# Regrouping the last units of a mixture-of-experts layer: three experts in the sixth unit, two on column tiles in the last, and the overflow branch moved

## The chip, the cores and the metric

The kernel runs on one core of a Trainium2 chip. The metric is the device time of one execution in microseconds. Before the change the median of three runs is 446.82 us (442.83, 446.82 and 448.70).

## What is computed

One decoder layer on 256 tokens of width 1024. A token mixer (sparse attention beside an mLSTM) and a layer norm come first. The change lies in the second half, the hierarchical mixture of experts, and in the last layer norm:

```python
for e in range(N_EXPERTS):                    # 16 experts, 1024 -> 512 -> 1024, f32
    hdn = jax.nn.silu(t @ w_gate[e]) * (t @ w_up[e])
    out = out + combine[:, e:e + 1] * (hdn @ w_down[e])   # combine: 0 but for a token's two experts
x = layer_norm(ALPHA * x + out, ln2_g, ln2_b)
```

Only two experts of each token have a weight above 0, so an expert's product needs only its own tokens.

## The kernel before

**Units.** After routing, the experts are ranked by how many tokens they have. Each gets a fixed number of rows, and experts are packed into units of 128 rows, one matmul output tile each. Units 1 and 2 hold experts 0 to 3 with 64 rows each. The other twelve experts follow `PLAN` in the order of `ORDER`: unit 3 has two experts of 64 rows, unit 4 four of 32, unit 5 one of 128, unit 6 four of 32, unit 7 one of 32. The constant `ALONE` marks the last. Tokens that do not fit in any of these rows are counted in `nex`; a loop behind a branch, `beyond()` (L1314), would compute them. In the runs shown its body does not run.

**One unit.** `onehot` (L1093, VectorE) builds the selection matrix OH from the token positions, `back` (L1134) transposes it (tile `poht`) and takes the routing weights (`pcw`), `gather` (L1115) multiplies the token matrix (a high and a low part, `x1h` and `x1l`, in fp32r) with OH and so collects the unit's tokens in `xg` (tile `pxg`). OH and `xg` are made for two units at a time. `gate` (L1171) makes `psg` and ScalarE's silu of it, `up_h` (L1184) makes `psu` and VectorE's `h`. `hidden_T` (L1195) transposes `h` (`pht`, `hT`), `down` (L1236) multiplies it with the down weights (`psd`) and writes two parts of `y`, and `combine` (L1250) scatters `y` back onto the tokens (`pcomb`) and adds it to the accumulator `x`. Each of the products of gate, up and down reads 2 MB of weights for each expert. A unit of four experts of 32 rows places each on its own column tile of TensorE, at output rows 0, 32, 64 and 96.

**The unit that stands alone.** With a single expert of 32 rows, three of four column tiles would be empty. `product_alone` (L1151) therefore splits the contraction instead: four slices of 128 input channels lie on the four column tiles at once (tile `pp`), and a product with the matrix `fold` adds the four partial sums (directly for the gate, after ScalarE's copy `part`; within the transpose for the rest). `down_part` (L1207) does the same with the hidden channels, in three cuts of the columns (`CUTS`: 512, 320 and 192), so that the sums for the last layer norm (`bn_stats`, tile `bst`) can start on the first cut.

**What sets the order.** Weights go through a ring of 20 slots of 1 MB. SyncE issues every load in the order of `loads_in_order`: for odd positions the gate weights of a unit, the down weights of the unit before it, then its up weights; for even positions down first. A load waits until the load eight places before it has landed, and until its slot is free. The down weights of the last unit are loaded by column cuts, 512 columns first, then 320, then 192. On TensorE the instructions run in the order in which the scheduler lists them. In the loop of L1358 a unit's `down` is placed behind the next unit's gate or gather. For the last unit, the order is: `combine` of unit 5, the branch `beyond()`, `onehot`, `back`, `gather` of 32 columns, and only then `down` of unit 6, whose `combine` comes at the end of the loop body.

Of the kernel before, what the change touches and what calls it, by code (L numbers as in the profile page):

```python
# [17 lines left out]
P = 128  # L18
D = 1024
KC = D // P  # L20
S = 256
# [8 lines left out]
PLAN = ((128,), (64, 64), (32, 32, 32, 32), (32, 32, 32, 32), (32,))  # L30
ORDER = (1, 2, 0, 3, 4)
ALONE = (32,)
# [27 lines left out]
def tile_layer(ctx: ExitStack, tc: tile.TileContext, x, w_in, cst, rows, toep, w_uk, w_uv,  # L60
# [1032 lines left out]
    def onehot(us):  # L1093

        OH = wk.tile([P, NB, 2 * P], F32R, tag="oh", name="oh")
        for u, (key, es, ws, pm, cm) in enumerate(us):
            if ws == ALONE:

                for b in range(NB):
                    nc.vector.tensor_scalar(OH[:, b, :P].rearrange("p (e j) -> p e j", e=4), iota1[:, :32].unsqueeze(1).to_broadcast([P, 4, 32]),  # L1100
                                            pm[:, b, 0:1], None, op0=ALU.is_equal)
# [13 lines left out]
    def gather(OH, n, kcs=range(KC), xg=xg):  # L1115

        for k0 in kcs[::2]:
            ps = tp_tile("pxg").rearrange("p (k t) -> p k t", k=2)
            for k in range(2):
                for i, (b, part) in enumerate(((0, x1h), (0, x1l), (1, x1h), (1, x1l))):  # L1120
                    nc.tensor.matmul(ps[:, k, :n], part[:, b, (k0 + k) * P:(k0 + k + 1) * P], OH[:, b, :n],  # L1121
                                            start=i == 0, stop=i == 3)
# [10 lines left out]

    def back(OH, u, unit):  # L1134

        cm = unit[4]
        us = slice(u * P, (u + 1) * P)
        pt = tp_tile("poht")
        for b in range(NB):
            nc.tensor.transpose(pt[:, b * P:(b + 1) * P], OH[:, b, us].bitcast(F32), ident)  # L1140
        OHT = wk.tile([P, S], F32R, tag="sc", name="oht", bufs=2)
        nc.scalar.copy(OHT, pt[:, :S])  # L1142
        pc = sm_tile("pcw")
        for b in range(NB):
            nc.tensor.matmul(pc[:, 0:len(unit[1])], OH[:, b, us].bitcast(F32), cm[:, b, :], start=b == 0, stop=b == 1)
        cw = wk.tile([P, 1], F32, tag="cw", name="cw", bufs=2)
        for i, ss, _ in ((0, slice(0, P), {}),) if unit[2] == ALONE else slots(unit):
# [23 lines left out]
    def gate(unit, u, psg=None):  # L1171
        if unit[2] == ALONE:
            part = wk.tile([P, 512], F32, tag="w2", name="part", bufs=2)
            nc.scalar.copy(part, product_alone(unit, 0))
# [5 lines left out]
        sg = wk.tile([P, 512], F32, tag="w2", name="sg", bufs=2)  # L1180
        nc.scalar.activation(sg, psg, AF.Silu)  # L1181
        return sg

    def up_h(unit, u, sg, cw):  # L1184
        if unit[2] == ALONE:
            psu = product_alone(unit, 1)
# [3 lines left out]
        h = wk.tile([P, 4, P], F32, tag="w2b", name="h", bufs=2)  # L1190
        nc.vector.scalar_tensor_tensor(h.rearrange("p j q -> p q j"), psu.rearrange("p (q j) -> p q j", j=4), cw[:, 0:1],  # L1191
# [3 lines left out]
    def hidden_T(h, alone=False):  # L1195
        pt = tp_tile("pht").rearrange("p (j t) -> p j t", j=4)
        for j in range(4):
            if alone:

                nc.tensor.matmul(pt[:, j, :], h[:, j, :], fold, start=True, stop=True)  # L1200
            else:
                nc.tensor.transpose(pt[:, j, :], h[:, j, :], ident)  # L1202
        hT = wk.tile([P, 4, P], F32, tag="hT", name="hT")
# [3 lines left out]
    def down_part(unit, hT, y, c0, n):  # L1207
# [12 lines left out]
    def y_parts(y, psd, c0, n):  # L1220
        ys = slice(c0, c0 + n)
        nc.scalar.copy(y[:, 0, ys], psd)  # L1222
        nc.vector.tensor_tensor(y[:, 1, ys], psd, y[:, 0, ys].bitcast(F32), op=ALU.subtract)  # L1223
# [12 lines left out]
    def down(unit, h):  # L1236
        hT, y = hidden_T(h), y_tile()
# [120 lines left out]
    for n, unit in enumerate(units):  # L1358
        if waits:
            if unit[2] == ALONE:  # L1360
# [16 lines left out]
        if n == 0:  # L1377
# [42 lines left out]
            fold_xg = wk.tile([P, P + KC * 32], F32, tag="wrs", name="fold_xg")  # L1420
            fold = fold_xg[:, :P]
            xga = fold_xg[:, P:].rearrange("p (k t) -> p k t", k=KC)
            nc.vector.tensor_reduce(fold[:, 0:32], ident.rearrange("p (i s) -> p s i", i=4), AX.X, ALU.add)
            nc.vector.tensor_copy(fold[:, 32:].rearrange("p (i s) -> p i s", i=3), fold[:, 0:32].unsqueeze(1).to_broadcast([P, 3, 32]))
        waits = (y, prev[2]) if n % 2 and n + 1 < NUNITS else None
        if prev and not waits:
# [99 lines left out]
```

## Time and profile before

| | before |
|---|---|
| median of 3 runs | 446.82 us |
| the profiled execution, device time | 444.41 us |
| its span | 442.7 us |
| TensorE busy | 419.2 us (95%) |
| VectorE busy | 226.1 us (51%) |
| ScalarE busy | 163.1 us (37%) |
| bytes moved | 137.28 MB, mean 310 GB/s |
| granted TensorE clock, mean | 0.972 of 2.4 GHz |

The profiled execution's own time, 444.41 us, is its span of 442.7 us and 1.7 us around it. PE stands for TensorE's matmuls, PEld for its weight loads, DVE for VectorE, ACT for ScalarE, SP for SyncE, whose queue issues the loads. A plain f32 matmul leaves two records in the trace, one of fp32r a single one. Ends of matmuls are modelled, so the records of a stream overlap; where a product's length matters, it is read from start to start.

### The profile page before, as it was taken

To read this page: it belongs to the slowest core of one execution; us is meant where nothing else is said; L and a number is where in the kernel's file an instruction comes from. 1 tells how busy PE (TensorE), PEld (TensorE's weight loads), DVE (VectorE), ACT (ScalarE), POOL (GpSimd) and SP (SyncE) were. 2 spreads that over 40 slices of the span, in tenths; PEclk is the share of its full clock that TensorE was granted. 3 is DMA by queue.
4 is the path that set the end of the run, shared out by engine and by line. 5 is a ranking of instruction groups with operands and counts; after the bars stand their busy time and mean duration, and the time that the engine had idled before them with its cause. 6 is when DMAs were issued, how large, how long until landed. Compare 5 with 4: busy or idle time off the path is not lost. (4 is left out here: it accounts for less than half of the span.)

```text
span 442.7 us, 7254 instructions
## 1 busy us (share of the span) xinstructions
PE 419.2 (95%) x2832; PEld 300.5 (68%) x2832; DVE 226.1 (51%) x493; ACT 163.1 (37%) x294; POOL 45.4 (10%) x74
## 2 busy tenths in 40 slices
PE   6999999999999999999999999999998999979980
PEld 6999996999999999999964434433334443426230
DVE  3698996499647756677582614204032202311247
ACT  4558556765766434454554011210112100101210
POOL 6326205041010001110000000000000000000001
PEclk8999999999999999999999999999999999995996
DMA  8973770796296878669687999999999999999962
GB/s 254 340 254 97 291 236 10 238 377 231 99 376 205 283 273 289 190 209 382 229 321 286 375 386 390 423 419 423 420 423 421 419 423 417 423 418 419 414 224 95
DMA packets 48519, 137.28 MB, mean 310 GB/s; under 512 B 3539, under 2 KB 32355, under 8 KB 36451
## 3 DMA queue, kind: packets, MB, share of 16 engines
q1 hardware_dynamic: 47394, 135.75, 81.0%
q10 hardware_dynamic: 1088, 1.05, 0.8%
q8 instruction: 23, 0.38, 0.4%
q14 instruction: 14, 0.11, 0.1%
HBM read 135.74 MB, written 1.05 MB: 309 GB/s over the span
## 5 line engine op out<-in xcount | busy, mean ns | idle before, releaser
L249 PE MATMUL accT<-xh,split 128*128 128x256 f32 (+1 forms) x264 | 75.6, 286 | 0.0
L253 PE MATMUL accT<-xh,split 128*128 128x256 f32 (+1 forms) x264 | 75.1, 284 | 0.3 <-DVE split L240 0.3
L252 PE MATMUL accT<-xl,split 128*128 128x256 f32 (+1 forms) x264 | 75.1, 284 | 0.0
L240 DVE TENSOR_TENSOR split<-raw,split 128x1024 fp32r<-128x1024 f32 (+2 forms) x52 | 63.9, 1234 | 18.4 <-ACT split L239 18.3
L239 ACT CAST split<-raw 128x1024 fp32r<-128x1024 f32 (+2 forms) x59 | 59.2, 1012 | 32.3 <-PE accT L253 10.1
L253 PEld LDWEIGHTS accT<-xh,split 128*128 128x128 f32 (+1 forms) x264 | 50.2, 190 | 0.5 <-DVE split L240 0.5
L249 PEld LDWEIGHTS accT<-xh,split 128*128 128x128 f32 (+1 forms) x264 | 50.2, 190 | 0.4 <-PE pl L589 0.2
L1243 PE MATMUL psd<-we,hT 128*32 128x512 f32 (+2 forms) x240 | 48.6, 638 | 1.7 <-ACT hT L1204 1.7
L252 PEld LDWEIGHTS accT<-xl,split 128*128 128x128 f32 (+1 forms) x264 | 50.2, 190 | 0.0
L1166 PE MATMUL psu<-we,xg 128*32 128x512 f32 (+2 forms) x240 | 47.3, 594 | 0.4 <-DMA we<-in_w_up_dram 0.4
L1166 PE MATMUL psg<-we,xg 128*32 128x512 f32 (+2 forms) x232 | 47.1, 596 | 0.0
L1223 DVE TENSOR_TENSOR y<-psd,y 128x512 fp32r<-128x512 f32 x12 | 8.3, 692 | 61.9 <-ACT y L1222 61.9
L1243 PEld LDWEIGHTS psd<-we,hT 128*32 128x32 f32 (+2 forms) x240 | 14.8, 132 | 30.8 <-issue 27.6
L1166 PEld LDWEIGHTS psu<-we,xg 128*32 128x32 f32 (+2 forms) x240 | 14.5, 126 | 28.9 <-issue 27.6
L1191 DVE SCALAR_TENSOR_TENSOR h<-psu,cw,sg 128x512 f32<-128x512 f32 x6 | 6.7, 1120 | 51.7 <-PE psu L1166 39.1
L1166 PEld LDWEIGHTS psg<-we,xg 128*32 128x32 f32 (+2 forms) x232 | 14.0, 125 | 24.1 <-issue 21.8
L1465 POOL TENSOR_TENSOR nm<-nm,nhalf 128x2 f32<-128x2 f32 x1 | 1.8, 1772 | 211.0 <-DVE nm L1466 211.0
L1142 ACT CAST oht<-poht 128x256 fp32r<-128x256 f32 x7 | 2.6, 371 | 53.6 <-PE pcomb L1229 28.3
L1222 ACT CAST y<-psd 128x512 fp32r<-128x512 f32 x12 | 7.0, 585 | 41.0 <-PE psd L1243 41.0
L1230 DVE TENSOR_TENSOR x<-x,pcomb 128x512 f32<-128x512 f32 (+2 forms) x30 | 17.9, 644 | 6.6 <-PE pcomb L1229 6.6
L240 POOL TENSOR_TENSOR split<-raw,split 128x1024 fp32r<-128x1024 f32 x7 | 17.5, 2505 | 20.0 <-ACT split L239 19.9
L1229 PE MATMUL pcomb<-y,oht 128*128 128x512 f32 (+2 forms) x60 | 18.6, 436 | 0.2 <-ACT y L1217 0.2
(356 smaller groups left out, 814.0 us busy)
## 6 DMA issues: line engine op xcount, KB each, us to landing
we<-in_w_up_dram SPq DMA_DIRECT2D x32, 1024.0 KB, 11.5
we<-in_w_gate_dram SPq DMA_DIRECT2D x31, 1024.0 KB, 11.1
we<-in_w_down_dram SPq DMA_DIRECT2D x31, 1024.0 KB, 15.2
raw<-in_w_in_dram SPq DMA_DIRECT2D x18, 1024.0 KB, 7.0
raw<-in_w_out_dram SPq DMA_DIRECT2D x4, 1024.0 KB, 4.9
raw<-in_w_up_a_dram SPq DMA_DIRECT2D x2, 1024.0 KB
raw<-in_w_up_m_dram SPq DMA_DIRECT2D x2, 1024.0 KB, 6.0
raw<-in_w_in_dram SPq DMA_DIRECT2D x2, 528.0 KB
```

The costliest lines, as they stand in the source:

```text
L239: a = nc.scalar.copy(hi, raw)
L240: b = (nc.gpsimd if pool else nc.vector).tensor_tensor(lo, raw, hi.bitcast(F32), op=ALU.subtract)
L249: i = nc.tensor.matmul(o, ah, bh, start=start, stop=False)
L252: nc.tensor.matmul(o, ah, bl, start=False, stop=False)
L253: return nc.tensor.matmul(o, al, bh, start=False, stop=stop)
L1166: last = nc.tensor.matmul(ps[ss, :], xg[:, kc, u * P + ss.start:u * P + ss.stop], wtiles[unit[0], wi, i, hf][kc % 4], start=kc == 0, stop= ...
L1191: nc.vector.scalar_tensor_tensor(h.rearrange("p j q -> p q j"), psu.rearrange("p (q j) -> p q j", j=4), cw[:, 0:1], sg.rearrange("p (q j) ...
L1222: nc.scalar.copy(y[:, 0, ys], psd)
L1223: nc.vector.tensor_tensor(y[:, 1, ys], psd, y[:, 0, ys].bitcast(F32), op=ALU.subtract)
L1229: i = [nc.tensor.matmul(pc, o, v, start=i == 0, stop=i == len(parts) - 1) for i, (o, v) in enumerate(parts)]
L1230: nc.vector.tensor_tensor(acc[:, b, ys], acc[:, b, ys], pc, op=ALU.add)
L1243: nc.tensor.matmul(psd[nh][ss, :], hT[:, j, ss], wtiles[unit[0], 2, i, hf][j % 2][:, nh * 512:nh * 512 + 512], start=j == 0, stop=j == 3, ...
```

## The change

Unit 6 holds three experts of 32 rows (96 rows; the gather of the pair of units 5 and 6 has 224 columns), and unit 7, the last, two experts of 32 rows. For it, `product_pair` lays two slices of the contraction of each of the two experts on the four column tiles (tile rows 0 and 32 for the first expert, 64 and 96 for the second), and `fold` adds the two slices. The down weights of the last unit are now six column cuts, two experts by three. In the loop, `down` and `combine` of unit 6 now come ahead of the branch, and the gather, of 64 columns, behind it.

```diff
-PLAN = ((128,), (64, 64), (32, 32, 32, 32), (32, 32, 32, 32), (32,))
+PLAN = ((128,), (64, 64), (32, 32, 32, 32), (32, 32, 32), (32, 32))
...
-    def product_alone(unit, wi):
+    def product_pair(unit, wi):
         pp = acc_tile("pp")
         for hf in range(2):
-            for k in range(4):
-                t = slice(k * 32, k * 32 + 32)
-                nc.tensor.matmul(pp[t, :], xga[:, hf * 4 + k, :], wtiles[unit[0], wi, 0, hf][k], start=hf == 0, stop=hf == 1,
-                                 tile_position=(0, k * 32))
-            consumed(1)
+            for k in range(0, 4, 2):
+                for i in range(2):
+                    for r in range(2):
+                        t = i * 64 + r * 32
+                        nc.tensor.matmul(pp[t:t + 32, :], xg[:, hf * 4 + k + r, i * 32:i * 32 + 32], wtiles[unit[0], wi, i, hf][k + r],
+                                         start=hf * 4 + k == 0, stop=hf * 4 + k == 6, tile_position=(0, t))
+            consumed(2)
...
-        for j in range(4):
-
-            t = slice(j * 32, j * 32 + 32)
-            i = nc.tensor.matmul(psd[t, :], hT[:, j, t], wtiles[unit[0], 2, 0, nh][j][:, o:o + n], start=True, stop=True, tile_position=(0, j * 32))
-            first = first or i
+        for j in range(0, 4, 2):
+            for e in range(2):
+                for r in range(2):
+
+                    q = e * 64 + r * 32
+                    i = nc.tensor.matmul(psd[q:q + 32, :], hT[:, j + r, q:q + 32], wtiles[unit[0], 2, e, nh][j + r][:, o:o + n],
+                                         start=j == 0, stop=j == 2, tile_position=(0, q))
+                    first = first or i
...
-            if unit[2] == ALONE:
+            if unit[2] == PAIR:
                 combine(*waits)
+                combine(down(*prev[:2]), prev[2])
                 beyond()
             OH = onehot(units[n:n + 2])
-            if unit[2] != ALONE:
+            if unit[2] != PAIR:
                 combine(*waits)
         OHT, cw = back(OH, n % 2, unit)
-        if waits and unit[2] == ALONE:
-            gather(OH, 32, xg=xga)
-        if waits:
+        if waits and unit[2] == PAIR:
+            gather(OH, 64, twice=True)
+        elif waits:
             y = down(*prev[:2])
-            if unit[2] != ALONE:
-                gather(OH, 2 * P)
+            gather(OH, P + rows_of(units[n + 1]))
```

On TensorE, around the branch. These are the rows before the change, from the up product of unit 6 (`psu`, four column tiles) to the branch on `nex`:

```order
L1243 MATMUL psd<-we,hT 128x512 x8
L1166 MATMUL psu<-we,xg 32x512
L1229 MATMUL pcomb<-y,oht 128x512 x8
L1166 MATMUL psu<-we,xg 32x512 x31
L1317 TENSOR_LOAD nex
L1320 COMPARE_AND_BRANCH
```

and these the rows of the same place now:

```order
L1258 MATMUL psd<-we,hT 128x512 x8
L1175 MATMUL psu<-we,xg 32x512
L1244 MATMUL pcomb<-y,oht 128x512 x8
L1175 MATMUL psu<-we,xg 32x512 x23
L1213 MATMUL pht<-ident,h 128x96 x4
L1258 MATMUL psd<-we,hT 32x512 x24
L1244 MATMUL pcomb<-y,oht 128x512 x8
L1332 TENSOR_LOAD nex
L1335 COMPARE_AND_BRANCH
```

The up product has 24 matmuls in place of 32, and the transpose, the down product and the eight `pcomb` of unit 6 moved in front of the branch.

On TensorE, behind the last gather. Before, `down` of unit 6 comes first (`pht`, `psd` of 32 matmuls), then the last unit's products (`pp`, `psg` by `fold`, `pht`, `psd` in cuts) with the `pcomb` of unit 6 between them:

```order
L1202 MATMUL pht<-ident,h 128x128 x4
L1243 MATMUL psd<-we,hT 32x512 x32
L1157 MATMUL pp<-we,fold_xg 32x512 x8
L1229 MATMUL pcomb<-y,oht 128x512 x4
L1176 MATMUL psg<-part,fold_xg 128x512
L1157 MATMUL pp<-we,fold_xg 32x512 x8
L1229 MATMUL pcomb<-y,oht 128x512 x4
L1200 MATMUL pht<-fold_xg,h 128x128 x4
L1215 MATMUL psd<-we,hT 32x512 x4
L1215 MATMUL psd<-we,hT 32x320 x4
L1229 MATMUL pcomb<-y,oht 128x512 x2
L1215 MATMUL psd<-we,hT 32x192 x4
```

and now:

```order
L1166 MATMUL pp<-we,xg 32x512 x16
L1185 MATMUL psg<-part,fold 128x512
L1166 MATMUL pp<-we,xg 32x512 x16
L1211 MATMUL pht<-fold,h 128x128 x4
L1228 MATMUL psd<-we,hT 32x512 x8
L1228 MATMUL psd<-we,hT 32x320 x8
L1244 MATMUL pcomb<-y,oht 128x512 x2
L1228 MATMUL psd<-we,hT 32x192 x8
```

Nothing of unit 6 stands behind the gather any more, and each product of the last unit has twice the matmuls.

On SyncE, the last weight loads ahead of the branch, before (the gate's second half, the two of up, the cuts of down; `ISA` computes an address):

```order
L130 DMA we<-in_w_gate_dram 128x2048
L130 ISA
L130 DMA we<-in_w_up_dram 128x2048
L130 ISA
L130 DMA we<-in_w_up_dram 128x2048
L130 ISA
L130 DMA we<-in_w_down_dram 128x4x512
L130 ISA
L130 DMA we<-in_w_down_dram 128x4x320
L130 ISA
L130 DMA we<-in_w_down_dram 128x4x192
```

and now, from the last load of up (four of gate and three of up stand ahead of it):

```order
L130 DMA we<-in_w_up_dram 128x2048
L130 ISA
L130 DMA we<-in_w_down_dram 128x4x512
L130 ISA
L130 DMA we<-in_w_down_dram 128x4x512
L130 ISA
L130 DMA we<-in_w_down_dram 128x4x320
L130 ISA
L130 DMA we<-in_w_down_dram 128x4x320
L130 ISA
L130 DMA we<-in_w_down_dram 128x4x192
L130 ISA
L130 DMA we<-in_w_down_dram 128x4x192
```

The number of bytes is the same; 12 MB instead of 6 MB belong to the last unit, and 4 MB instead of 2 MB come in column cuts.

## Rows read from the trace of the kernel before

**Rows 1.** Page part 2, 40 equal slices: granted clock, DMA share, GB/s
```profile
PEclk8999999999999999999999999999999999995996
DMA  8973770796296878669687999999999999999962
GB/s 254 340 254 97 291 236 10 238 377 231 99 376 205 283 273 289 190 209 382 229 321 286 375 386 390 423 419 423 420 423 421 419 423 417 423 418 419 414 224 95
```

**Rows 2.** Timeline of TensorE: start us, us, what, count [idle before]
```profile
306.91 7.07 PE L1166 MATMUL psg<-we,xg 128*32 128x512 f32 x62
313.91 0.66 PE L1202 MATMUL pht<-ident,h 128*128 128x128 f32 x4
...
352.97 7.03 PE L1166 MATMUL psg<-we,xg 128*128 128x512 f32 x16
359.83 7.03 PE L1166 MATMUL psu<-we,xg 128*128 128x512 f32 x16
...
376.39 7.13 PE L1243 MATMUL psd<-we,hT 128*128 128x512 f32 x16
383.46 1.04 PE L1166 MATMUL psu<-we,xg 128*32 128x512 f32 x2
384.43 2.24 PE L1229 MATMUL pcomb<-y,oht 128*128 128x512 f32 x8
386.61 4.49 PE L1166 MATMUL psu<-we,xg 128*32 128x512 f32 x36
391.48 3.62 PE L1166 MATMUL psu<-we,xg 128*32 128x512 f32 x26 [0.39 <-DMA we<-in_w_up_dram]
```

**Rows 3.** SyncE's issues of weight loads, timeline from 390 us
```profile
394.05 2.81 SPq L130 DMA_DIRECT2D we<-in_w_gate_dram  x2
399.01 2.81 SPq L130 DMA_DIRECT2D we<-in_w_up_dram  x2
403.96 14.17 SPq L130 DMA_DIRECT2D we<-in_w_down_dram  x3
424.16 0.85 SPq L1460 DMA_DIRECT2D lnr<-in_rows_dram  x2
```

**Rows 4.** Line 130 from 380 us: down loads, ns each, first and last start
```profile
L130 SPq DMA_DIRECT2D we<-in_w_down_dram x8: 333/333/8788, 381.6 to 409.3; - x8
```

**Rows 5.** Page part 6: the loads of the two later cuts, KB, us to landing
```profile
we<-in_w_down_dram SPq DMA_DIRECT2D x1, 640.0 KB, 19.2
...
we<-in_w_down_dram SPq DMA_DIRECT2D x1, 384.0 KB, 17.3
```

**Rows 6.** Timeline of TensorE, last unit: waits for its gate and up weights
```profile
416.31 0.30 PEld L1157 LDWEIGHTS pp<-we,fold_xg 128*32 128x32 f32 x8 [0.56 <-DMA we<-in_w_gate_dram]
...
419.43 1.07 PE L1157 MATMUL pp<-we,fold_xg 128*32 128x512 f32 x8
421.30 1.07 PE L1157 MATMUL pp<-we,fold_xg 128*32 128x512 f32 x8 [0.80 <-SPq L1320]
```

**Rows 7.** The chain that ended last, by time (extract): start us, us, what
```profile
397.90 6.85 PE pxg L1121 x32
404.75 0.97 PE pht L1202 x4
...
406.43 9.37 PE psd L1243 x64
415.81 1.72 PE pp L1157 x16
...
422.49 1.15 DVE h L1191
423.68 1.17 PE pht L1200 x8
...
425.56 1.11 PE psd L1215 x8
```

**Rows 8.** Timeline of VectorE: adds, h, one-hot, and the first add of the end
```profile
385.20 2.48 DVE L1230 TENSOR_TENSOR x<-x,pcomb 128x512 f32<-128x512 f32 x4 [0.33 <-PE pcomb L1229]
395.14 1.10 DVE L1191 SCALAR_TENSOR_TENSOR h<-psu,cw,sg 128x512 f32<-128x512 f32 x1 [7.46 <-PE psu L1166]
396.55 0.48 DVE L1100 TENSOR_SCALAR oh<-iota,pmP 128x128 fp32r<-128x128 f32 x2 [0.31 <-DVEq L1320]
...
428.50 0.69 DVE L1230 TENSOR_TENSOR x<-x,pcomb 128x512 f32<-128x512 f32 x1 [3.77 <-PE pcomb L1229]
```

**Rows 9.** Windows: stretch, us, busy of PE, PEld, DVE, ACT, POOL, clock, DMA, GB/s
```profile
396.00:397.00 1.00, 0.02 (x1) 0.05 (x1) 0.69 (x3) 0.00 (x0) 0.00 (x0) 1.00 0.99 401
397.00:398.00 1.00, 1.00 (x8) 1.00 (x8) 0.09 (x2) 0.37 (x1) 0.00 (x0) 0.73 0.96 401
...
411.00:412.00 1.00, 1.00 (x12) 0.24 (x8) 0.00 (x0) 0.00 (x0) 0.00 (x0) 0.94 0.94 393
```

**Rows 10.** Timeline of TensorE: gather of 256 columns, first and last of seven matmuls
```profile
339.08 0.28 PE L1121 MATMUL pxg<-oh,x1l 128*128 128x256 f32 x1
...
339.79 0.28 PE L1121 MATMUL pxg<-oh,x1l 128*128 128x256 f32 x1
```

**Rows 11.** Groups by form from 240 us (busy us, mean ns): weight loads of column tiles
```profile
L1166 PEld LDWEIGHTS psu<-we,xg 128*32 128x32 f32 x128 | 4.4, 109 | 11.9 <-issue 10.6 <-DMA we<-in_w_up_dram 1.3
```

More of the change, by code (lines that the diff above doesn't have):

```diff
@@ L1113, in scaled, with gather, of @@
                 nc.vector.tensor_scalar(xg[:, k + 1, :n], odd, ln1gq[:, k + 1:k + 2], ln1bq[:, k + 1:k + 2], op0=ALU.mult, op1=ALU.add))
-    def gather(OH, n, kcs=range(KC), xg=xg):
+    def gather(OH, n, kcs=range(KC), twice=False):
+        def of(b):
+            return OH[:, b, :2 * n].rearrange("p (e i j) -> p e i j", e=2, i=2)[:, :, 0, :] if twice else OH[:, b, :n]
         for k0 in kcs[::2]:
@@ L1132, in slots, with rows_of @@
             q += w
+    def rows_of(unit):
+        return P if unit[2] == PAIR else sum(unit[2])
     def back(OH, u, unit):
-        cm = unit[4]
-        us = slice(u * P, (u + 1) * P)
+        cm, r = unit[4], rows_of(unit)
+        us = slice(u * P, u * P + r)
         pt = tp_tile("poht")
         for b in range(NB):
-            nc.tensor.transpose(pt[:, b * P:(b + 1) * P], OH[:, b, us].bitcast(F32), ident)
-        OHT = wk.tile([P, S], F32R, tag="sc", name="oht", bufs=2)
-        nc.scalar.copy(OHT, pt[:, :S])
+            nc.tensor.transpose(pt[:r, b * P:(b + 1) * P], OH[:, b, us].bitcast(F32), ident)
+        OHT = wk.tile([P, S], F32R, tag="sc", name="oht", bufs=2)[:r]
+        nc.scalar.copy(OHT, pt[:r, :S])
         pc = sm_tile("pcw")
         for b in range(NB):
-            nc.tensor.matmul(pc[:, 0:len(unit[1])], OH[:, b, us].bitcast(F32), cm[:, b, :], start=b == 0, stop=b == 1)
+            nc.tensor.matmul(pc[:r, 0:len(unit[1])], OH[:, b, us].bitcast(F32), cm[:, b, :], start=b == 0, stop=b == 1)
         cw = wk.tile([P, 1], F32, tag="cw", name="cw", bufs=2)
-        for i, ss, _ in ((0, slice(0, P), {}),) if unit[2] == ALONE else slots(unit):
+        for i, ss, _ in [(i, slice(i * 64, i * 64 + 64), {}) for i in range(2)] if unit[2] == PAIR else slots(unit):
             nc.vector.tensor_copy(cw[ss, :], pc[ss, i:i + 1])
         return OHT, cw
-    def product_alone(unit, wi):
+    def product_pair(unit, wi):
         pp = acc_tile("pp")
         for hf in range(2):
-            for k in range(4):
-                t = slice(k * 32, k * 32 + 32)
-                nc.tensor.matmul(pp[t, :], xga[:, hf * 4 + k, :], wtiles[unit[0], wi, 0, hf][k], start=hf == 0, stop=hf == 1,
-                                 tile_position=(0, k * 32))
-            consumed(1)
+            for k in range(0, 4, 2):
+                for i in range(2):
+                    for r in range(2):
[3 more added lines that the diff above has]
+            consumed(2)
         return pp
@@ L1171, in gate @@
     def gate(unit, u, psg=None):
-        if unit[2] == ALONE:
+        if unit[2] == PAIR:
             part = wk.tile([P, 512], F32, tag="w2", name="part", bufs=2)
-            nc.scalar.copy(part, product_alone(unit, 0))
+            nc.scalar.copy(part, product_pair(unit, 0))
             psg = acc_tile("psg")
@@ L1179, in gate @@
             product(psg, unit, 0, u)
-        sg = wk.tile([P, 512], F32, tag="w2", name="sg", bufs=2)
-        nc.scalar.activation(sg, psg, AF.Silu)
+        sg = wk.tile([P, 512], F32, tag="w2", name="sg", bufs=2)[:rows_of(unit)]
+        nc.scalar.activation(sg, psg[:rows_of(unit)], AF.Silu)
         return sg
     def up_h(unit, u, sg, cw):
-        if unit[2] == ALONE:
-            psu = product_alone(unit, 1)
+        if unit[2] == PAIR:
+            psu = product_pair(unit, 1)
         else:
@@ L1221, in y_parts @@
         ys = slice(c0, c0 + n)
-        nc.scalar.copy(y[:, 0, ys], psd)
-        nc.vector.tensor_tensor(y[:, 1, ys], psd, y[:, 0, ys].bitcast(F32), op=ALU.subtract)
+        r = y.shape[0]
+        nc.scalar.copy(y[:, 0, ys], psd[:r])
+        nc.vector.tensor_tensor(y[:, 1, ys], psd[:r], y[:, 0, ys].bitcast(F32), op=ALU.subtract)
     def combine_part(y, OHT, b, c0, n):
@@ L1236, in down @@
     def down(unit, h):
-        hT, y = hidden_T(h), y_tile()
+        hT, y = hidden_T(h), y_tile()[:rows_of(unit)]
         psd = [acc_tile("psd") for _ in range(2)]
@@ L1418, in tile_layer @@
                             nc.vector.scalar_tensor_tensor(acc[:, b, ns], pgb, ALPHA, acc[:, b, ns], op0=ALU.mult, op1=ALU.add)
[L1420 to L1424, printed above, removed]
+            fold = wk.tile([P, P], F32, tag="wrs", name="fold")
+            fv, iv = (t.rearrange("p (e r j) -> p e r j", e=2, r=2) for t in (fold, ident))
+            for r in range(2):
+                nc.vector.tensor_tensor(fv[:, :, r, :], iv[:, :, 0, :], iv[:, :, 1, :], op=ALU.add)
         waits = (y, prev[2]) if n % 2 and n + 1 < NUNITS else None
-        if prev and not waits:
+        if prev and not waits and unit[2] != PAIR:
             combine(y, prev[2])
```

28 lines of the change are left out of this document (15 added, 13 removed).

## The prediction

> **What bounds the kernel now.** I read the page's slices first. From the 26th slice to the 38th the DMA engines are full at about 420 GB/s [rows 1], so from some 277 us on (25 slices of 11.07 us) the weights arrive at a fixed pace, and only an idle stretch of the queue could move their end. Next I read who waits at the end. TensorE works without a gap up to 391 us, where unit 6's up product waits 0.39 us for its weights [rows 2]. The last unit's gate product then waits for a load that lands at 416.3, its up product for one that lands at 421.3 [rows 6]. Two loads of 1 MB between these give 2.5 us a load. SyncE is far ahead: it issues these loads between 394 and 410 [rows 3], the last cut at 409.3 [rows 4], and that lands 17.3 later [rows 5], at 426.6. Behind 421.3 comes a chain that waits for no load: the second half of up to 422.4, `h`, the transpose by `fold`, `psd` at 425.56 [rows 6, 7], the first add into the accumulator at 428.50 [rows 8]. From there to the end VectorE's adds and the layer norm take what they take, unchanged. So the change is worth what it does to that first add.
>
> One more thing is to be seen. The granted clock is 1.2 GHz from 397.7 to about 411.1 [rows 9]. Ahead of the fall TensorE stood idle from 395.1 to 397.0, and then came the gather, whose 32 matmuls of 32 columns took 6.85 us [rows 7]. Ahead of the rise it had run `psd` since 406.43. This cost nothing much, because the loads were late anyway. It is what I fear for the new order.
>
> **When the weights land now.** The bytes are the same. Before, the last 4 MB took 10.3 us (416.3 to 426.6). Now all 4 MB come in cuts; by the price of the two that do now (421.3 to 426.6) that is 10.6, so the last cut lands at 426.9, up's last load at 416.3, the 512-column cuts by 422 and the 320s by 425. Counting back by 2.5 us, the gate's four are in at 406.3, unit 6's down weights at 396.3, its up weights at 381.3. Now it is TensorE that is late.
>
> **TensorE's path, at full clock.** Lengths are read from start to start.
> - Up product of unit 6. A product of four column tiles takes 7.0 us (306.91 to 313.91 for 62 of 64 records), one of full width 6.9 [rows 2]: sixteen passes of 512 columns set the time, not the number of tiles. Three experts cost as much as four. From 386.6: 393.6, and no wait for weights. Before, `h` began at 395.14 [rows 8]: 1.5 gained.
> - `h` 1.1, then transpose and copy 1.7 (404.75 to 406.43 [rows 7]), then `psd` 7.0: 403.4. Its weights came by 396.3.
> - `y`, eight `pcomb`, four adds. For unit 5 the adds end at 387.7, 4.2 us behind `psd` at 383.5, with 1.0 of another product between [rows 2, 8]: 3.2, so 406.6. Nothing covers this now, since the branch and the one-hot stand behind the adds in VectorE's order.
> - Branch, one-hot, transposes: from the end of `h` at 396.24 to the gather at 397.90 it was 1.7; two more one-hot instructions of 0.24 [rows 8] make 2.2: 408.8.
> - Gather: 32 matmuls, spaced 0.118 us at full clock with 256 columns [rows 10]. With 64 they are no faster than that by any row, so 3.8: 412.6.
> - Gate: 32 records instead of 16, at 7.0 for 62: 3.6, to 416.2. Copy and `fold` as before, 1.9 (417.5 to 419.43 [rows 6, 7]): 418.1. Up 3.6: 421.7; its last load was there at 416.3.
> - `h`, transpose, copy to `psd` as before, 3.2 (422.37 to 425.56): 424.9. From `psd` to the first add 2.9 as before, and 1.5 for sixteen more records in the first two cuts (0.9 for eight of 512, 0.6 of 320): 429.3.
>
> That is 0.8 us behind 428.50. The gather of units 5 and 6 with 224 columns, and the operations on 96 rows, save at most some tenths; I count them as nothing.
>
> **The clock.** TensorE is thinly used from 403.4 to 412.6 (eight `pcomb` with a gap, 1.7 us idle, then the gather), and this stretch lies on the path. Bounds: it keeps the full clock, 0; or it fares as before, the whole gather at 6.85 (3.05 more), and of the gate's product as long a piece at half speed as of the old `psd`, 406.43 to 411.1 (2.35 more): 5.4. The nearest row is the old gather, which ran at 1.2 GHz throughout; but here a dense `psd` of 7 us and the `pcomb` stand closer ahead, and the idle time is 0.2 shorter. I take 1.7, about a third.
>
> Sum: 444.41 + 0.8 + 1.7 = 446.9 for an execution like the profiled one. The three runs of before lie from 1.6 under it to 4.3 over it, with their median 2.4 over. I add 1.0 and forecast **447.9**.
>
> **A rule against the change.** In a product of four column tiles 62 matmuls with as many weight loads take 7.0 us, a product of full width with 16 takes 6.9 [rows 2], so loads of 0.109 us each [rows 11] hide. The Trainium skill, in "TensorE: Matmul & The Clock Gate", section "Part 3: Packing small matmuls — row/col tiling", says that a weight load overlaps running matmuls only where the row group differs; column tiles all share theirs. By the rows the 28 matmuls added to gate, up and the three cuts cost their passes alone, which is in the sum. By the rule their 28 weight loads would come on top, 3.1 us.
>
> **Rivals.**
> - *The loads decide after all, and the clock holds (0.27).* My joins between streams may be too long by a tenth each. If TensorE keeps pace, the 320s at 425 and the last cut at 426.9 set the end: `psd` of the 320s to about 426.0, first add about 427.0, so 1.5 better: 442.9, with the 1.0 as above 443.9. For it: the queue is full all the time. Against it: the sum has up's product 3.6 us behind its weights.
> - *The low clock lasts as long as before (0.17).* 444.41 + 0.8 + 5.4 = 450.6, with 1.0: 451.6. For it: the old gather. Against it: unlike then, the work ahead and behind is dense.
> - *The 224 columns cost the plain f32 price (0.06).* No row shows fp32r between 32 and 256 columns. A plain f32 record of 512 columns takes 0.43 us (6.9 for 16), a matmul leaves two, so 224 columns would take 0.375 instead of 0.118: 8.2 us over 32 matmuls at about 340 us. TensorE has no gap from there to 391, and the path above begins with it, so all of it would reach the end: 446.9 + 8.2 + 1.0 = 456.1, slower by over 2%. It decides from a loss of some 9 us in all. Against it: 32 columns took 0.214 (6.85 by 32) at half the clock, 256 take 0.118 at full clock, nearly the same number of its cycles, which looks like a floor and not like a price by columns.
> - *The added weight loads don't hide (0.05).* 28 at 0.109 make 3.1: 451.0. For it the rule above; against it the products in [rows 2].
>
> My forecast has 0.45.
>
> **Range and chances.** The likeliest case alone spans 445 to 451. The range 442.5 to 453.0 takes in the first two rivals and the last, and the spread of single runs; it leaves out the third. A difference of 2% (8.9 us) is about what a measurement of this kernel can tell from no change. Slower by more than that comes from the third rival, 0.06; faster has no case, 0.01; within 2% it is 0.93.
>
> **What the profile of the changed kernel will show.** Right: `h` of unit 6 starts near 393.7, its `psd` ends near 403.4, the last gather starts near 408.8; the last unit's gate and up products start without waiting for weights; the granted clock shows a stretch at 1.2 GHz between 404 and 420; the first cut's add lies between 428 and 433. Wrong: a wait for weights in the last unit's up product (then the loads still decide); a gather of 224 columns spaced more than 0.15 us; a slice of the DMA share under 9 tenths between 330 and 420 us, where I have assumed the ring's slots to come free in time.

## The result, and the profile after

| | before | after |
|---|---|---|
| median | 445.19 us (5 runs, 442.83 to 448.70) | 458.05 us (5 runs, 455.05 to 458.63) |
| the profiled execution | 444.41 us | 455.05 us |
| its span | 442.7 us | 453.4 us |
| TensorE busy | 419.2 us | 428.8 us |
| VectorE busy | 226.1 us | 226.0 us |
| granted TensorE clock, mean | 0.972 | 0.973 |

The changed kernel is slower: the ratio to the kernel before is 1.0264, 95% interval 1.022 to 1.0308. The forecast was 447.9 us with a range to 453.0. The two profiled executions differ by 10.7 us of span, and those 10.7 us are what the traces explain; the medians differ by 12.9, because the profiled execution of after happens to be the lowest of its five.

All 10.7 us are there at the first add into the accumulator, which now starts at 439.21 instead of 428.50 [rows 8]. From there to the end nothing changed. So I walk back from it. First VectorE in the timeline of after, the rows that answer to [rows 8]:

```profile
398.01 1.09 DVE L1201 SCALAR_TENSOR_TENSOR h<-psu,cw,sg 96x512 f32<-96x512 f32 x1 [6.06 <-PE psu L1175]
...
408.72 2.47 DVE L1245 TENSOR_TENSOR x<-x,pcomb 128x512 f32<-128x512 f32 x4
411.64 0.74 DVE L1101 TENSOR_SCALAR oh<-iota,pmP 128x64 fp32r<-128x64 f32 x4 [0.45 <-DVEq L1335]
...
439.21 0.69 DVE L1245 TENSOR_TENSOR x<-x,pcomb 128x512 f32<-128x512 f32 x1 [6.04 <-PE pcomb L1244]
```

`h` of unit 6 was forecast for 393.7 and comes at 398.01: 4.3 us are lost already, before any of the stages that I had costed with care. From there to the one-hot the forecast's lengths hold (adds end 13.2 us behind `h`; forecast 12.9).

The 4.3 us come from the down product of unit 4, at 337 us. This is TensorE in the timeline of after, each piece of that product with the row behind it (`x8` counts records, two for each matmul):

```profile
336.93 1.92 PE L1258 MATMUL psd<-we,hT 128*32 128x512 f32 x8 [0.51 <-ACT hT L1215]
338.78 0.37 PE L1124 MATMUL pxg<-oh,x1h 128*128 128x224 f32 x1
...
339.86 1.90 PE L1258 MATMUL psd<-we,hT 128*32 128x512 f32 x4
341.70 0.37 PE L1124 MATMUL pxg<-oh,x1h 128*128 128x224 f32 x1
...
342.78 3.62 PE L1258 MATMUL psd<-we,hT 128*32 128x512 f32 x20
346.33 0.37 PE L1124 MATMUL pxg<-oh,x1h 128*128 128x224 f32 x1
...
352.35 3.65 PE L1258 MATMUL psd<-we,hT 128*32 128x512 f32 x24
355.93 1.57 PE L1244 MATMUL pcomb<-y,oht 128*128 128x512 f32 x5
```

Two more pieces of `x4` start at 346.86 and 349.32 and take 1.83 and 1.84. And the same product before, in three pieces (the gather resumes at 338.63 and 343.71, and `pcomb` starts at 351.71):

```profile
336.78 1.92 PE L1243 MATMUL psd<-we,hT 128*32 128x512 f32 x8
341.88 1.90 PE L1243 MATMUL psd<-we,hT 128*32 128x512 f32 x4
344.72 7.05 PE L1243 MATMUL psd<-we,hT 128*32 128x512 f32 x52
```

The reader is to see that a piece of two matmuls takes as long as one of four, and one of 26 as long as a whole product of 32. The order of instructions in the two programs, with the output rows of each matmul, tells why. The scheduler doesn't list the 32 matmuls in rounds over the four column tiles; it often puts both output halves of one expert, which is one tile, behind each other. Where gather matmuls of full width cut in, what follows can't fill the empty tiles. So a piece lasts as long as the tile with the most matmuls in it. I call these its turns; a turn is 0.857 us (352.97 to 359.83 for eight matmuls [rows 2]).

| kernel, piece | matmuls | on tiles 0, 1, 2, 3 | turns | start of the piece to start of the next row, us |
|---|---|---|---|---|
| before, 1 | 4 | 2, 2, 0, 0 | 2 | 1.85 |
| before, 2 | 2 | 0, 0, 2, 0 | 2 | 1.83 |
| before, 3 | 26 | 6, 6, 6, 8 | 8 | 6.99 |
| after, 1 | 4 | 2, 2, 0, 0 | 2 | 1.85 |
| after, 2 | 2 | 0, 0, 2, 0 | 2 | 1.84 |
| after, 3 | 10 | 2, 2, 2, 4 | 4 | 3.55 |
| after, 4 | 2 | 2, 0, 0, 0 | 2 | 1.83 |
| after, 5 | 2 | 0, 2, 0, 0 | 2 | 1.84 |
| after, 6 | 12 | 2, 2, 4, 4 | 4 | 3.58 |

Twelve turns before, 16 after; 8 would do. In time: 10.67 and 14.49 us, 3.8 more, of the 4.2 by which the next unit's gate product now starts later (357.33 against 352.97, less 0.16 by which the trace of after was already late ahead of this product). Why the scheduler lists the gather of 224 columns among the pieces in this way isn't shown.

The other loss is the clock. Stretches of 1 us in after, the rows that answer to [rows 9] (columns: us, busy of PE, PEld, DVE, ACT, POOL, clock, DMA share, GB/s):

```profile
411.00:412.00 1.00, 0.00 (x0) 0.00 (x0) 0.55 (x4) 0.00 (x0) 0.00 (x0) 0.94 1.00 418
412.00:413.00 1.00, 0.80 (x5) 0.75 (x5) 0.38 (x3) 0.06 (x1) 0.00 (x0) 0.50 0.98 410
425.00:426.00 1.00, 1.00 (x12) 0.16 (x4) 0.00 (x0) 0.00 (x0) 0.00 (x0) 0.73 0.78 251
426.00:427.00 1.00, 0.55 (x8) 0.00 (x0) 0.00 (x0) 0.37 (x1) 0.00 (x0) 1.00 0.41 134
```

The clock is 1.2 GHz from near 412 to past 425. TensorE stood idle ahead of it, as before. The chain of work that ended last, in order of time, shows what ran at half speed:

```profile
412.20 0.71 PE poht L1147 x2
412.91 0.65 PE pcw L1152 x4
413.55 6.88 PE pxg L1124 x32
420.43 6.18 PE pp L1166 x32
...
428.39 3.62 PE pp L1166 x32
...
435.12 3.00 PE psd L1228 x32
```

The gather took 6.88 where 3.8 was forecast for full clock, the gate's `pp` 6.18 where the same 32 records of up took 3.62: 3.1 and 2.6, together 5.6 us; the sum had 1.7. Loads play no part any more: nothing in this chain waits for one. The three parts, 4.2 (turns and what goes with them), 5.6 (clock) and the 0.8 of the forecast's own account, make 10.6 of the 10.7.

### The profile page after: what moved, and what is told of

It reads as the page before. It is cut to its first block, busy times and chain, and to the rows that moved or that the text cites. A ratio compares the mean times of both kernels' runs of the same rounds, so it can differ in the third digit from the quotient of the medians.

```text
span 453.4 us, 7283 instructions
## 1 busy us (share of the span) xinstructions
PE 428.8 (95%) x2840; PEld 302.9 (67%) x2840; DVE 226.0 (50%) x495; ACT 163.2 (36%) x294; POOL 45.4 (10%) x74
## 5 line engine op out<-in xcount | busy, mean ns | idle before, releaser
L1258 PE MATMUL psd<-we,hT 128*32 128x512 f32 (+2 forms) x224 | 50.4, 596 | 2.1 <-ACT hT L1215 2.1
L1175 PE MATMUL psu<-we,xg 128*32 128x512 f32 (+2 forms) x224 | 46.3, 594 | 0.0
L1238 DVE TENSOR_TENSOR y<-psd,y 128x512 fp32r<-128x512 f32 (+1 forms) x12 | 8.3, 691 | 56.9 <-ACT y L1237 56.9
L1201 DVE SCALAR_TENSOR_TENSOR h<-psu,cw,sg 128x512 f32<-128x512 f32 (+1 forms) x6 | 6.7, 1119 | 50.4 <-PE psu L1175 37.7
L1237 ACT CAST y<-psd 128x512 fp32r<-128x512 f32 (+1 forms) x12 | 7.0, 586 | 35.4 <-PE psd L1258 35.4
L1244 PE MATMUL pcomb<-y,oht 128*128 128x512 f32 (+3 forms) x60 | 19.3, 443 | 0.1
L1114 DVE TENSOR_SCALAR xg<-pxg,cst_sb 128x256 f32<-128x256 f32 (+2 forms) x14 | 6.7, 477 | 25.4 <-ACT xg L1113 25.4
## 6 DMA issues: line engine op xcount, KB each, us to landing
we<-in_w_gate_dram SPq DMA_DIRECT2D x31, 1024.0 KB, 10.7
```

What stands on the lines that cost most here:

```text
L1175: last = nc.tensor.matmul(ps[ss, :], xg[:, kc, u * P + ss.start:u * P + ss.stop], wtiles[unit[0], wi, i, hf][kc % 4], start=kc == 0, stop= ...
L1238: nc.vector.tensor_tensor(y[:, 1, ys], psd[:r], y[:, 0, ys].bitcast(F32), op=ALU.subtract)
L1244: i = [nc.tensor.matmul(pc, o, v, start=i == 0, stop=i == len(parts) - 1) for i, (o, v) in enumerate(parts)]
L1258: nc.tensor.matmul(psd[nh][ss, :], hT[:, j, ss], wtiles[unit[0], 2, i, hf][j % 2][:, nh * 512:nh * 512 + 512], start=j == 0, stop=j == 3, ...
```

## Experiments

Theory 1: the broken down product of unit 4 costs. Theory 2: the low clock at the last gather costs. Theory 3: the doubled matmuls of the last unit cost, or the moved branch by itself. Times of the kernel before beside these runs were 444.5 to 445.0 us.

### The down product in one piece

```diff
-            gather(OH, P + rows_of(units[n + 1]))
+            gather(OH, P + rows_of(units[n + 1]), behind_=psd_last[0] if n == 4 else None)
```

(Every gather matmul is listed behind the last `psd`. The `pcomb` of unit 5 keep their place within the up product of unit 6.)

> The changed kernel, with one thing undone: the 32 down matmuls of the unit at 336 us (four column tiles) run in one piece, and the 32 gather matmuls of 224 columns behind them, in place of six pieces with gather matmuls between. Theory 1 (each break of a column-tile product by full-width matmuls costs about 1 us; six pieces took 14.5 us from start to start where a whole product takes 7.0, the kernel before paid 10.7 for three): the next unit's gate product starts near 350 us instead of 357.3, and the end comes about 7 us earlier, about 451 us against 458. Theory 2 alone (the loss is the low clock around the last gather, 411.9 to 425.3 us): less than 1 us, about 458. Theory 3 (the doubled matmuls of the last unit, or the place of the branch): 458 too.

Measured: 450.38 us, 1.0124 (1.008 to 1.0169) of before. That is 7.7 us under the changed kernel. Theory 1 holds: 16 turns against 8. The execution that was profiled is 4.7 us above this median (its down product of unit 4 took 8.82 us, at a granted clock of 0.83 from 340 to 350 us), so I read the lengths from the run with both edits, below, which has the product in one piece too:

```profile
338.04 7.13 PE L1271 MATMUL psd<-we,hT 128*32 128x512 f32 x64 [0.73 <-ACT hT L1226]
345.10 0.37 PE L1124 MATMUL pxg<-oh,x1h 128*128 128x224 f32 x1
...
375.48 7.13 PE L1271 MATMUL psd<-we,hT 128*128 128x512 f32 x16 [0.73 <-ACT hT L1226]
```

The product itself takes 7.06 instead of 14.49 us, 7.4 less. TensorE's path gains less: from the start of unit 4's down product to the start of unit 6's it is 63.40 us in the changed kernel (336.93 to 400.33) and 57.08 here (338.04 to 395.12), 6.3 less, chiefly because in the new order the transposes of unit 5 are followed by a wait of 0.73 us for their copy `hT` (the last row), which other work covered before. The rest of the 7.7 between the medians is not shown by a trace; the five times of the changed kernel alone lie between 455.05 and 458.63. Theory 3 has no part in this gain.

### TensorE kept busy around the last gather

```diff
-            return OH[:, b, :2 * n].rearrange("p (e i j) -> p e i j", e=2, i=2)[:, :, 0, :] if twice else OH[:, b, :n]
+            return OH[:, b, :P].unsqueeze(1).to_broadcast([P, 2, P]) if twice else OH[:, b, :n]
...
-                    nc.tensor.matmul(ps[:, k, :n], part[:, b, (k0 + k) * P:(k0 + k + 1) * P], of(b),
+                    nc.tensor.matmul(ps[:, k, :].rearrange("p (r t) -> p r t", r=2) if twice else ps[:, k, :n], part[:, b, (k0 + k) * P:(k0 + k + 1) * P], of(b),
...
+            if unit[2] == PAIR:
+                pw4 = sm_tile("warm4")
+                for i in range(3):
+                    w4 = nc.tensor.matmul(pw4, ident, x1h[:, 0, :512].bitcast(F32), start=True, stop=True)
             OH = onehot(units[n:n + 2])
```

> The changed kernel, with TensorE kept busy around the last gather: three plain matmuls of 512 columns (results unused) fill its idle 2 us behind the branch, and each gather matmul streams 256 columns (the same 128 columns twice) instead of 64. Theory 2 (the 1.2 GHz from 411.9 to 425.3 us costs about 3.0 us in the gather and 2.6 in the gate's product): the granted clock stays at 2.4 GHz, the gather takes 3.8 us instead of 6.9, the gate 3.6 instead of 6.2, and the time falls by 4 to 5.5 us, to about 453. Theory 1 alone: no change at the end, 458. If the clock falls all the same, the time is 458 to 459 and theory 2 stays open.

Measured: 453.29 us, 1.0187 (1.0142 to 1.0231), 4.8 under the changed kernel. TensorE's timeline of this run:

```profile
408.70 2.82 PE L1250 MATMUL pcomb<-y,oht 96*128 96x512 f32 x8
412.85 2.84 PE L1388 MATMUL warm<-x1h,ident 128*128 128x512 f32 x6 [1.34 <-DVEq L1341]
...
416.12 0.36 PE L1124 MATMUL pxg<-oh,x1h 128*128 128x256 f32 x1
...
420.37 3.64 PE L1172 MATMUL pp<-we,xg 128*32 128x512 f32 x32
```

The gather now takes 4.25 us (416.12 to 420.37) and the gate's `pp` 3.64. So theory 2 holds too. The first row shows what the edit didn't foresee: `pcomb` starts at 408.70, 8.74 behind the start of the down product of unit 6 at 399.96. In the changed kernel it was 7.04 (400.33 to 407.37):

```profile
400.33 7.11 PE L1258 MATMUL psd<-we,hT 128*32 128x512 f32 x48 [0.62 <-ACT hT L1215]
407.37 2.82 PE L1244 MATMUL pcomb<-y,oht 96*128 96x512 f32 x8
```

The granted clock of the run with the edit was 0.66 from 400 to 405.

### Half of that edit: the wide gather alone

The same without the three dummies.

> The changed kernel with only one half of the edit that kept the clock: each matmul of the last gather streams 256 columns instead of 64, and nothing fills TensorE's idle 2 us ahead of it. If the idle time behind the branch is what lets the clock fall: it falls as before, the gather's matmuls are spaced 0.2 us or more, and the time is 457 to 459. If the narrow gather matmuls are what lets it fall: the clock stays at 2.4 GHz, the spacing is 0.118 us, and the time is about 453, or 452 since no dummy stands ahead of the transposes.

Measured: 452.66 us, 1.0153 (1.0101 to 1.0206): the time that I had put down to the second case, by a course that neither case had. The clock falls behind the idle time all the same, but is back near 420 us, within the gather:

```profile
414.52 0.56 PE L1124 MATMUL pxg<-oh,x1h 128*128 128x256 f32 x1
414.88 0.41 PE L1124 MATMUL pxg<-oh,x1l 128*128 128x256 f32 x1
...
420.25 0.29 PE L1124 MATMUL pxg<-oh,x1h 128*128 128x256 f32 x1
420.37 0.28 PE L1124 MATMUL pxg<-oh,x1l 128*128 128x256 f32 x1
...
420.82 3.64 PE L1172 MATMUL pp<-we,xg 128*32 128x512 f32 x32
```

The first matmuls are spaced 0.21 us as at 64 columns, the last ones 0.12, and the gate's product runs at 2.4 GHz. In the changed kernel the clock returned only after the whole gather and some 5 us of that product. So in the trace the saving is the gate's 2.6 us and some 0.6 at the end of the gather, 3.2 of the 5.4 between the medians. The profiled execution, 454.67, is the highest of its four: it was 1.1 us late already ahead of unit 4's down product, and lost 1.7 more at the end, where `psd` of the first cuts took 4.70 instead of 3.00 us at a granted clock of 0.84 and 0.82 (430 to 435 and 435 to 440 us). The dummies bring no more than they cost: 453.29 with them, 452.66 without.

### Both edits together

> The changed kernel with both edits: the down product at 336 us in one piece, and TensorE kept busy around the last gather. Theories 1 and 2 together: the savings add up, 7 and 5, to about 446 us, at which the weight loads (the last cut lands near 426.5 us) decide again; the last unit's up product then waits little or not at all. If the two savings share a cover (the loads, or the clock falling earlier when the path is earlier): 448 to 452. If the doubled matmuls of the last unit are the cost: above 455.

Measured: 447.13 us, 1.0032 (0.9996 to 1.0068). Of 458.05 that is 10.9 off, where the single savings were 7.7 and 4.8. Here too the down product of unit 6 took longer:

```profile
395.12 8.81 PE L1271 MATMUL psd<-we,hT 128*32 128x512 f32 x48 [0.62 <-ACT hT L1226]
```

and the stretches of 5 us say that it was the clock, which is back at full in the next one:

```profile
395.00:400.00 5.00, 4.88 (x24) 1.50 (x25) 0.00 (x0) 0.07 (x1) 0.00 (x0) 0.66 1.02 421
400.00:405.00 5.00, 5.00 (x34) 1.93 (x28) 1.07 (x2) 1.16 (x2) 0.00 (x0) 1.00 1.00 416
```

So the two savings add up but for 1.6 us, and theory 3 is out as a cost beyond what the two edits undo: the doubled matmuls and the moved branch are all in this kernel, which is within 0.7% of before. What the move costs through the idle time behind the branch and the low clock belongs to theory 2.

### The kernel before, with the move alone

```diff
                 combine(*waits)
+                combine(down(*prev[:2]), prev[2])
                 beyond()
...
-        if waits:
+        if waits and unit[2] != ALONE:
             y = down(*prev[:2])
-            if unit[2] != ALONE:
-                gather(OH, 2 * P)
+            gather(OH, 2 * P)
```

> The kernel before, with the move alone: down and combine of unit 6 ahead of the branch, the gather of the last unit behind it; the plan stays (four experts of 32 rows in unit 6, one in unit 7). From the rows of before: h of unit 6 at 396.2, down product to 405, adds to 408, gather from 410 to 414 at full clock or 417 at 1.2 GHz, gate by 418 to 420, up behind its load of 421.3 or from 422. Theories 1 and 2: the move alone costs 0 to 2 us here (445 to 448), because the loads of the last unit, which land at 416 and 421 us, hide most of it. Theory 3 in its form that the move of the branch is the cost: 453 or more.

Measured: 458.86 us, 1.0301 (1.0256 to 1.0345). Theories 1 and 2, as I had applied them here, missed this by over 10 us, and the number is one that I had put down to theory 3. The trace shows another course than a price of the branch. TensorE's timeline of this run (the profiled execution, 462.16, is the highest of its five), the down product of unit 6:

```profile
399.43 3.17 PE L1243 MATMUL psd<-we,hT 128*32 128x512 f32 x12 [0.73 <-ACT hT L1204]
403.18 4.39 PE L1243 MATMUL psd<-we,hT 128*32 128x512 f32 x24 [0.58 <-DMA we<-in_w_down_dram]
408.14 1.90 PE L1243 MATMUL psd<-we,hT 128*32 128x512 f32 x4 [0.57 <-DMA we<-in_w_down_dram]
410.63 1.90 PE L1243 MATMUL psd<-we,hT 128*32 128x512 f32 x4 [0.59 <-DMA we<-in_w_down_dram]
413.12 3.62 PE L1243 MATMUL psd<-we,hT 128*32 128x512 f32 x20 [0.59 <-DMA we<-in_w_down_dram]
```

I had let it start at 398 and run 7 us. But in the old plan its weights are four experts', eight loads, and only the last unit's 6 MB come behind them, so they land near the end: SyncE issues the last of the eight at 393.3, it lands 19.8 us later, at 413.1, and the last pieces start 2.5 us apart, as the loads land. Each landing lets two matmuls of one expert go, a piece of two turns on one tile (1.90 us). The product ends at 416.7. Then the adds, the branch, the one-hot and a gather at 1.2 GHz follow in line (422.0 to 430.8). In the kernel before, this product stood behind the gather, at 406.43, and did not wait for a load [rows 7]. In the new plan 12 MB come behind the down weights of unit 6; the last of them is issued at 377.4 in the changed kernel, and by the same 19.8 us it is in near 397, ahead of the product at 400.33. So the move is cheap only with the new plan; the two edits can't be judged one without the other.

### The same six pieces, cut at whole rounds

```diff
+            if n == 4:
+                row = []
+                for g, p in ((2, 4), (8, 4), (8, 8), (3, 4), (4, 4), (7, 8)):   # gather, then down matmuls
+                    row += [pxgs.pop(0) for _ in range(g)] + [psds.pop(0) for _ in range(p)]
+                for one, two in zip(row, row[1:]):
+                    after(one, two)
```

> The changed kernel with its six pieces of the down product at 336 us kept, and the same groups of gather matmuls between them (2, 8, 8, 3, 4, 7), but the pieces cut at whole rounds over the four column tiles: 4, 4, 8, 4, 4, 8 matmuls, each piece as many on every tile; now they are 4, 2, 10, 2, 2, 12, with 2, 2, 4, 2, 2, 4 on the fullest tile. Theory 1a (a piece lasts as long as its fullest column tile, 0.853 us a matmul and 0.17 more; 16 turns in the changed kernel, 8 when whole): 8 turns and six times 0.17 make 7.9 us, 0.8 more than in one piece, so about 451 us. Theory 1b (each return from full-width matmuls to column tiles costs about 1 us by itself, whatever is in the piece): six times 0.98 and eight times 0.865 make 12.8, 5.7 more than in one piece, so about 456 us.

Measured: 450.33 us, 1.0105 (1.0049 to 1.016), with as many breaks as the changed kernel. TensorE's timeline:

```profile
336.72 1.07 PE L1260 MATMUL psd<-we,hT 128*32 128x512 f32 x8 [0.51 <-ACT hT L1217]
337.72 0.37 PE L1126 MATMUL pxg<-oh,x1h 128*128 128x224 f32 x1
...
340.88 1.92 PE L1260 MATMUL psd<-we,hT 128*32 128x512 f32 x16
342.73 0.37 PE L1126 MATMUL pxg<-oh,x1h 128*128 128x224 f32 x1
```

Four matmuls on four tiles take 1.00 us; the same number on two tiles took 1.85. The six pieces together last 7.68 us, against 14.49 in the changed kernel and 7.06 in one piece. It is the empty tiles that cost, not the breaks: theory 1a. The Trainium skill, in "TensorEngine Tiling (Array Packing)", section "Tiling Modes", says that changing the tiling mode drains TensorE. These rows agree that leaving the column tiles and coming back costs something, 0.62 us for six pieces in place of one, and put the size at some 0.1 us a piece; that it is a drain, no run here shows.

### The kernel before, with its down product in one piece

The edit of the first experiment, in the kernel before.

> The kernel before with its down product at 336 us in one piece (now three pieces, 12 turns of the fullest tile instead of 8). Theory 1 saves about 3.6 us of TensorE's time there too. In this kernel the weight loads set the end (the last unit's gate and up products wait for loads that land at 416.3 and 421.3), so if the account holds that the loads decide before and TensorE after, the time hardly moves: 443.5 to 445.5. If TensorE decided before as well: about 441.5.

Measured: 445.20 us, 1.0004 (0.9969 to 1.0039). The time that TensorE saves at 336 us is spent waiting for the up weights of unit 6, 0.50 and 1.44 us where before it was 0.39 [rows 2]:

```profile
389.21 1.05 PE L1168 MATMUL psu<-we,xg 128*32 128x512 f32 x2 [0.50 <-DMA we<-in_w_up_dram]
391.69 3.62 PE L1168 MATMUL psu<-we,xg 128*32 128x512 f32 x26 [1.44 <-DMA we<-in_w_up_dram]
```

So the loads decide in the kernel before, and four wasted turns cost nothing there. In the changed kernel, where TensorE decides, eight wasted turns cost, as the first experiment shows.

### Whole rounds elsewhere, and the clock kept without delay

```diff
-                after(ups_[0], combs[-4][0])
-                after(combs[-1][-1], ups_[1])
+                after(ups_[2], combs[-4][0])
+                after(combs[-1][-1], ups_[3])
...
-                combine(down(*prev[:2]), prev[2])
+                combine(down(*prev[:2], fill_=True), prev[2])
+                fill(combs[-1][-1], 2)
                 beyond()
...
-            if unit[2] == PAIR:
-                pw4 = sm_tile("warm4")
-                for i in range(3):
-                    w4 = nc.tensor.matmul(pw4, ident, x1h[:, 0, :512].bitcast(F32), start=True, stop=True)
```

(`ups_` are the up matmuls of unit 6, `combs` the `pcomb`. The gate product and `pcw` are ordered in the same way. `fill` lists dummies behind an instruction.)

> The kernel of the run with both edits (down product in one piece, TensorE kept busy around the last gather), with three more edits of the same two kinds. The gate and up products of unit 6, on three column tiles, give way to other matmuls only after a whole round of three instead of after one (each lone matmul now costs a turn of 0.85 us). Two dummies stand ahead of the branch instead of three behind it, where they delayed the transposes by about 1.5 us. One dummy fills TensorE's wait for the h of unit 6, ahead of the down product that ran in part at 1.2 GHz (8.81 instead of 7.1 us). By the theory of turns 1.7 us, by the dummies' place 1.5, by the clock 1.7: the first add moves from 431.8 to about 427, where the loads set the end: about 443.5 us, at or just under the kernel before. If the clock falls somewhere else: 445 to 447.

Measured: 443.48 us, 0.9961 (0.9937 to 0.9985): 0.4% faster than the kernel before, and 14.6 us under the changed one. The three edits were made together, so the run doesn't tell what each is worth. TensorE's timeline:

```profile
381.23 2.24 PE L1256 MATMUL pcomb<-y,oht 128*128 128x512 f32 x8
383.40 6.21 PE L1186 MATMUL psu<-we,xg 128*32 128x512 f32 x42
...
392.05 7.17 PE L1279 MATMUL psd<-we,hT 128*32 128x512 f32 x48 [0.62 <-ACT hT L1227]
...
409.47 3.64 PE L1175 MATMUL pp<-we,xg 128*32 128x512 f32 x32
...
424.61 1.27 PE L1240 MATMUL psd<-we,hT 128*32 128x320 f32 x12 [0.49 <-SPq L1356]
```

and VectorE's first add of the end:

```profile
426.98 0.69 DVE L1257 TENSOR_TENSOR x<-x,pcomb 128x512 f32<-128x512 f32 x1 [7.24 <-PE pcomb L1256]
```

The rest of up now takes 6.21 instead of 7.06, the down product of unit 6 its full-clock length, and the first add comes at 426.98, 1.5 us before that of [rows 8]. A `psd` of the 320 columns now stands behind a wait of 0.49 us, put down to an instruction of SyncE that had long run; as with the last wait of [rows 6], the landing of its weights fits. So the loads seem to set the pace again, and the first add comes where the forecast's first rival, in which the loads decide, had put it (427.0).

### The gather ahead of the down product, without the loop

```diff
                 combine(*waits)
-                combine(down(*prev[:2]), prev[2])
-                beyond()
...
             gather(OH, 64, twice=True)
+            y = down(*prev[:2])
```

> The changed kernel without the branch and its overflow loop, and with that the order that the kernel before had: one-hot and gather of the last unit ahead of the down product of unit 6 (with the branch between them the ring's 20 slots don't hold what must be loaded ahead of it, so this order can only be had without the loop). The 32 gather matmuls of 64 columns now stand inside the gate product of unit 6, which they cut into pieces of 1, 1, 10, 1, 1 and 10 matmuls on three column tiles. If the place behind the branch were the whole loss beyond the 4.2 us at 336: no idle time and no low clock at the gather, the first add some 10 us earlier, about 447 us. By the rule of turns as well: the gate product has 12 turns instead of 9, the up product 10 instead of 9, 3.4 us and some 0.8 for the pieces more; the first add comes at about 434 instead of 439, so about 453 us.

Measured: four runs of 453.6, 459.6, 460.6 and 461.7 us, beside a before of 444.46; the ratio is 1.0274 (1.0174 to 1.0373), more than no change, but unclear against 2%. None came near the 447 of the first case. The lowest is what the rule of turns gave, the other three are 6 to 8 us above it, which no case foresaw. The profiled execution is the highest of the four, and the lowest has no trace, so the difference stays unexplained. The run shows that the order of the kernel before can't be had back for nothing: the edit breaks the gate product of unit 6 as the change broke the down product of unit 4. What the place behind the branch costs by itself it can't tell.

## Why the prediction was wrong

**What bounds the kernel before: right.** The run with its down product in one piece shows it: TensorE's gain turns into waits for loads. (That TensorE works without a gap up to 391 us is a slip: it waits 1.23 us for `h` at 335 and 0.29 at 340. Nothing in the sum hangs on it.)

**When the weights land: right as far as the sum needs it.** The change's chain waits for none, and the loads stay at 418 to 424 GB/s up to 408 us. None of the three signs of being wrong that the forecast named appeared; what missed were its start times, from `h` of unit 6 on.

**The step that failed** stands in the last sentence on TensorE's path: "The gather of units 5 and 6 with 224 columns, and the operations on 96 rows, save at most some tenths; I count them as nothing." The path was started "From 386.6", a time taken over from the trace of before, as if nothing moved ahead of it. I looked at the price of a gather matmul and not at where the 32 stand. The order of instructions showed three pieces of the product of unit 4 before and six now, and [rows 2] held the price of a turn. Four more turns at 0.857 and three more pieces at some 0.12 make 3.8 us; measured 3.8, with 0.4 beside it.

**The term that was mis-sized** is the clock: 1.7 taken, "about a third" of the way between 0 and 5.4; measured 5.6. The nearest row, the old gather at 1.2 GHz throughout, was named there and then discounted because a dense product stood closer ahead and the idle time was 0.2 shorter (it came to 2.01 us, 1.88 before). The clock fell all the same. The rival with the low clock as long as before was right on the clock, at 451.6, and like the forecast it lacked the turns; with the 4.2 of the failed step it would have stood at 455.8.

**What held.** The branch, one-hot and adds behind `h` of unit 6 took what the sum said. The third rival fell: gather matmuls of 224 columns are spaced 0.11 us. The rival of weight loads that don't hide fell: the up product of unit 6 takes 7.06 with three tiles, and the 32 records of the last unit's up product 3.62 at full clock. Its price was worked out wrong, too: the trace has two weight loads for each matmul (eight for four in [rows 6]), so the 28 added matmuls bring 56 loads, 6.1 us at 0.109 each and not 3.1; that would have put it at 454.0. The rule of the Trainium skill that stood against the change ("TensorE: Matmul & The Clock Gate", "Part 3: Packing small matmuls — row/col tiling") isn't borne out for column tiles here: 31 matmuls on four column tiles, with 62 loads of 0.109 us, 6.8 us in all, take 7.0 us [rows 2, 11].

**What stays open.** I can't say why the clock fell for a while within a dense product on column tiles. The down product of unit 6 took 8.81 us in some of the profiled executions and 7.11 in others, the changed kernel's among them. It doesn't seem to go by the kernel alone: of the ten executions with both edits, the two lowest (443.9 us) have a mean granted clock of 0.991 and the two highest (449.8) one of 0.978 and 0.979. This may also be the 2.2 us between the difference of the medians and that of the profiled executions: the two lowest executions of the changed kernel (455.05 and 456.11) have a mean clock of 0.973, the two highest (458.29 and 458.63) 0.966, and 0.007 of 455 us is 3.2 us, an estimate of mine, as much as lies between them. The two highest have no trace that could show where they lost it.

## What to carry to other kernels

Where small matmuls share TensorE by column tiles, count each uninterrupted piece by its fullest tile, in the order that the scheduler lists, and let other work in only at whole rounds; a change far away can break such a product anew. A time taken over from the old trace as the start of a sum has to be earned: compare the order of instructions up to that point first. And when the nearest row of the trace is one bound of a cost, a discount from it needs a row too.

## What was not expected of the hardware

A piece of an f32 product on column tiles, 512 columns wide, between full-width matmuls takes 0.857 us times the matmuls on its fullest tile and some 0.1 us more: two matmuls on one tile 1.84, four on two tiles 1.85, four on four tiles 1.00. And the last gather's matmuls are spaced the same with 64 and with 256 columns, 0.21 us at the low clock (at 2.4 GHz 0.12 with 256, and 0.11 with 64, where the run without the loop has such rows: 376.17 to 376.62 us). Yet with 256 the clock, which fell in both, was back at 2.4 GHz near 420 us and the gate's product took 3.64 us; with 64 it came back past 425 and the product took 6.18.
